# The last store of a router kernel, issued as two halves of the partitions by two engines

## The chip, the cores and the metric

The kernel runs on one core of a Trainium2 chip. The metric is the device time of one execution in microseconds; less is better. The profile's span, from the first to the last instruction of the core, is somewhat shorter than that time, because the time also holds what surrounds the program.

A core has engines with instruction streams of their own: TensorE (PE) for matrix products and transposes, VectorE (DVE), ScalarE (ACT), GpSimd (POOL) and SyncE (SP). They hand work to each other through semaphores. SyncE, ScalarE and GpSimd can issue DMA transfers between the large memory (DRAM) and the on-chip memory, which has 128 partitions. The transfers are carried out by the core's 16 DMA engines, and a transfer raises a semaphore by 16 in all when it has landed.

## The reference

A softmax over eight logits per row of a large input:

```python
# x: [16, 512, 1024] float32, router_weights: [1024, 8] float32
def reference(x, router_weights):
    logits = np.matmul(x, router_weights)
    exp_logits = np.exp(logits - np.max(logits, axis=-1, keepdims=True))
    return (exp_logits / np.sum(exp_logits, axis=-1, keepdims=True)).astype(np.float32)
```

There are 16 x 512 = 8192 rows. The input has 33.5 MB, the output 8192 x 8 floats, which is 256 KB.

## The kernel before

The 8192 rows are laid out as 128 partitions times 64 columns (`J`): partition `p` holds rows `64 p` to `64 p + 63`. So a column `j` is one row of each partition, and a partition's results for neighbouring columns are neighbours in DRAM.

```python
x_rows = x.rearrange("b s d -> (b s) d").rearrange("(p j) d -> p j d", p=P)      # P = 128
out_rows = out.rearrange("b s n -> (b s) n").rearrange("(p j) n -> p j n", p=P)  # J = 64, N = 8
...
outv = sb("outv", [P, J, N], fp32)      # all results, on chip
...
s_st = [sem(f"s_st{i}") for i in range(2)]
```

The input comes in by loads issued by GpSimd, after two issued by SyncE and the weights issued by ScalarE at the very start:

```python
nc.sync.dma_start(
    out=x_f32[:, 2 * i:2 * i + 2, :], in_=x_rows[:, 2 * i:2 * i + 2, :]
).then_inc(s_f[i], 16)                                    # line 131, i = 0 and 1
...
nc.scalar.dma_start(
    out=w8, in_=router_weights.rearrange("(ko ki) n -> ko ki n", ko=KO)
).then_inc(s_w, 16)                                       # line 137, KO = 8 rows of 4 KB
```

For each column TensorE transposes the eight 128 x 128 blocks of x, VectorE and ScalarE copy the turned blocks out of the accumulation memory, and TensorE multiplies them with the weights. The softmax is done by VectorE and ScalarE for groups of eight columns. The last four columns (`ALONE = 4`) are done one by one, so that the work after the last load is short; their sum, reciprocal and scaling are the last three instructions of VectorE. The scaling writes the last results to `outv` and raises `s_out` for the last time, to `NG + 1`.

```python
# ScalarE, at the end of its list
def power_alone(k):
    act.wait_ge(s_low, k + 1)
    act.activation(
        ev3[:, k, :], alone[k], func=Exp, bias=low[:, k:k + 1]
    ).then_inc(s_e3, 1)                                   # line 342
...
for k in range(ALONE):
    power_alone(k)

# VectorE, at the end of its list
dve.wait_ge(s_e3, ALONE)
dve.reduce_sum(sum3[:, :, 0], ev3, axis=X).then_inc(s_d, 1)               # line 441
dve.wait_ge(s_d, 3 * (NG) + 1)
dve.reciprocal(inv3, sum3).then_inc(s_d, 1)                               # line 443
dve.wait_ge(s_d, 3 * (NG) + 2)
dve.tensor_tensor(
    out=outv[:, J - ALONE:J, :], in0=ev3, in1=inv3.broadcast_to([P, ALONE, N]), op=ALU.mult
).then_inc(s_out, 1)                                                      # line 445
```

SyncE passes on, for each column, that its input has landed (line 157). After that it stores the results in two parts, and waits until both have landed. The first part is columns 0 to 51 (`DONE` = 52), the last part columns 52 to 63: 12 x 8 floats, 384 bytes, from each of the 128 partitions, 48 KB in all.

```python
sp.wait_ge(s_out, NG - 1)
sp.dma_start(out=out_rows[:, 0:DONE, :], in_=outv[:, 0:DONE, :]).then_inc(s_st[0], 16)   # line 160
sp.wait_ge(s_out, NG + 1)
sp.dma_start(out=out_rows[:, DONE:J, :], in_=outv[:, DONE:J, :]).then_inc(s_st[1], 16)   # line 162
for s in s_st:
    sp.wait_ge(s, 16)                                                                    # line 164
```

Of the kernel before, what the change touches and what calls it, by code (L numbers as in the profile page):

```python
# [11 lines left out]
def kernel(  # L12
# [7 lines left out]
    P = 128  # L20
# [5 lines left out]
    J = M // P  # L26
# [3 lines left out]
    out_rows = out.rearrange("b s n -> (b s) n").rearrange("(p j) n -> p j n", p=P)  # L30
# [15 lines left out]
    NG = (J - ALONE + SKIP) // G  # L46
    starts = [max(0, G * g - SKIP) for g in range(NG)]
    ends = [G * (g + 1) - SKIP for g in range(NG)]
    DONE = ends[-2]
# [5 lines left out]
    def sb(name, shape, dtype):  # L55
        size = mybir.dt.size(dtype)
        for n in shape[1:]:
            size *= n
        at = place[0]
        place[0] = -(-(at + size) // 64) * 64  # L60
        return nc.alloc_sbuf_tensor_at(name, shape, dtype, offset=at).ap()
# [11 lines left out]
    outv = sb("outv", [P, J, N], fp32)  # L73
# [22 lines left out]
    sem = tc.alloc_semaphore  # L96
# [23 lines left out]
    s_low = sem("s_low")  # L120
    s_e3 = sem("s_e3")
    s_out = sem("s_out")
    s_st = [sem(f"s_st{i}") for i in range(2)]

    first = [sum(LOADS[:i]) for i in range(len(LOADS))]
    cols = [sum(PIECES[:i]) for i in range(len(PIECES))]
# [2 lines left out]
    with tc.manual_schedule():  # L129
        early = [  # L130
            nc.sync.dma_start(
                out=x_f32[:, 2 * i:2 * i + 2, :], in_=x_rows[:, 2 * i:2 * i + 2, :]
            ).then_inc(s_f[i], 16)
            for i in range(2)
# [3 lines left out]
                out=w8, in_=router_weights.rearrange("(ko ki) n -> ko ki n", ko=KO)  # L138
# [8 lines left out]
    sp = nc.sync  # L147
# [11 lines left out]
    sp.wait_ge(s_out, NG - 1)  # L159
    sp.dma_start(out=out_rows[:, 0:DONE, :], in_=outv[:, 0:DONE, :]).then_inc(s_st[0], 16)  # L160
    sp.wait_ge(s_out, NG + 1)
    sp.dma_start(out=out_rows[:, DONE:J, :], in_=outv[:, DONE:J, :]).then_inc(s_st[1], 16)
    for s in s_st:
        sp.wait_ge(s, 16)

# [1 line left out]
    for i, r in enumerate(LOADS):  # L167
        if i:
            nc.gpsimd.dma_start(  # L169
                out=xa[:, first[i]:first[i] + r, :], in_=x_rows[:, first[i]:first[i] + r, :]  # L170
            ).then_inc(s_ld[i], 16)
        if i == 2:
# [3 lines left out]
                out=ident, in_=ident, compare_op=ALU.not_equal, fill=1.0, base=0,  # L176
# [151 lines left out]
    act = nc.scalar  # L328
# [11 lines left out]
# [4 lines that stand above are left out]
        ).then_inc(s_e3, 1)  # L344
# [16 lines left out]
    act.copy(xTz[0], z_bank[0]).then_inc(s_zc[0], 1)  # L361
    for k in range(ALONE):
        power_alone(k)


    dve = nc.vector
# [52 lines left out]
    for j in range(J - 3):  # L419
# [26 lines left out]
        out=outv[:, J - ALONE:J, :], in0=ev3, in1=inv3.broadcast_to([P, ALONE, N]), op=ALU.mult  # L446
# [31 lines left out]
```

## Time and profile before

| What | Value |
|---|---|
| time, median of 3 runs | 87.13 us (87.0 to 87.17) |
| span in the profile | 85.7 us |
| busy share of the span: TensorE, VectorE, ScalarE, GpSimd | 74%, 45%, 44%, 16% |
| read from and written to DRAM | 33.59 MB and 0.26 MB |
| first store: size, from issue to landing | 208 KB, 1.9 us |
| last store: size, from issue to landing | 48 KB, 1.6 us |
| DMA packets of SyncE's queue (q1) and ScalarE's queue (q10) | 576 and 16 |

The page of a profile shows the span in 40 slices with one digit for each, the busy share in tenths. "DMA" is the mean busy share of the 16 DMA engines. The chain that ended last is followed back from the last instruction. A row of a table by stretches begins with its window in microseconds and its length; then come busy time and instruction counts of TensorE's multiplier, its weight loads, VectorE, ScalarE and GpSimd, the granted clock of TensorE, the mean busy share of the DMA engines, and the rate in GB/s. "SPq" and "ACTq" are the queues of instructions of SyncE and ScalarE, in which DMA issues stand; the length of an issue is not that of the transfer. A number after L is a line of the kernel.

### The profile page before, as it was taken

Reading aid. Unit: us, or ns where it says so; the run is one execution under the profiler, and the core shown is the slowest. Engines: PE = TensorE matmul, PEld = TensorE weight load, DVE = VectorE, ACT = ScalarE, POOL = GpSimd, SP = SyncE. Lnnn points to the kernel's source line nnn. Section 1 sums busy time; section 2 is a strip of 40 time slices with the busy share of each in tenths; the row PEclk is TensorE's granted clock in tenths of the full one; section 3 lists DMA queues with packets and bytes.
Section 4 is the critical chain, followed back from the end, with each engine's and each line's share of the span. In section 5 each row is a group of like instructions: output and inputs, shape, how many; then the busy total and the mean of one; then the engine's idle time right before and its main releaser. Section 6 shows DMA issues by size and latency. Waiting matters only on the chain. (4 is left out here: it accounts for less than half of the span.)

```text
span 85.7 us, 2847 instructions
## 1 busy us (share of the span) xinstructions
PE 63.7 (74%) x1094; PEld 52.0 (61%) x1094; DVE 38.9 (45%) x114; ACT 38.1 (44%) x81; POOL 13.4 (16%) x30
## 2 busy tenths in 40 slices
PE   0052639999998986959496895959597799999860
PEld 0040637888886764838475673837475588776740
DVE  0020222447467452745256362636256267664661
ACT  0029386246556262535245252525336256555370
POOL 0489999800000000000000000000000000000000
PEclk9999999999999999999999999999999999999995
DMA  3899999999999999999999999999999999999920
GB/s 50 337 417 318 218 203 226 210 222 210 222 207 226 203 226 207 230 199 230 199 230 214 218 210 218 222 210 218 210 218 197 216 212 214 200 211 209 163 99 23
DMA packets 3906, 18.14 MB, mean 212 GB/s; under 512 B 568, under 2 KB 1080, under 8 KB 2112
## 3 DMA queue, kind: packets, MB, share of 16 engines
q0 software_dynamic: 3312, 15.73, 89.9%
q1 hardware_dynamic: 576, 2.36, 7.3%
q10 hardware_dynamic: 16, 0.03, 0.4%
q14 instruction: 2, 0.02, 0.0%
HBM read 33.59 MB, written 0.26 MB: 395 GB/s over the span
## 5 line engine op out<-in xcount | busy, mean ns | idle before, releaser
L348 ACT COPY xTs<-pts 128x384 bf16<-128x384 bf16 x63 | 30.2, 479 | 38.0 <-PE pts L276 36.7
L374 DVE COPY xTv<-ptv 128x640 bf16<-128x640 bf16 x63 | 31.0, 492 | 34.1 <-PE ptv L276 29.8
L276 PE MATMUL ptv<-identity,x_all 128*128 128x128 bf16 x311 | 28.7, 225 | 13.1 <-SPq L157 8.8
L276 PEld LDWEIGHTS ptv<-identity,x_all 128*128 (+1 forms) x311 | 18.9, 99 | 14.4 <-issue 14.3
L276 PE MATMUL pts<-identity,x_all 128*128 128x128 bf16 x186 | 21.3, 225 | 0.0
L263 PEld LDWEIGHTS lg<-w_bf,xTv 128*128 128x128 bf16 x305 | 15.6, 98 | 7.9 <-issue 1.5
L263 PE MATMUL spare<-filler 128*128 128x512 bf16 x61 | 19.5, 401 | 0.6
L263 PE MATMUL lg<-w_bf,xTv 128*128 128x8 bf16 x305 | 16.6, 167 | 0.0
L276 PEld LDWEIGHTS pts<-identity,x_all 128*128 x186 | 13.6, 101 | 0.0
L263 PE MATMUL lg<-w_bf,xTs 128*128 128x8 bf16 x183 | 13.2, 166 | 0.0
L169 POOL DMA_DIRECT2D x_all<-in_x_dram x20 | 10.7, 607 | 2.8 <-POOLq L144 2.8
L263 PEld LDWEIGHTS lg<-w_bf,xTs 128*128 128x128 bf16 x183 | 8.9, 96 | 0.0
L263 PEld LDWEIGHTS spare<-filler 128*128 128x128 bf16 x61 | 4.5, 101 | 2.5 <-issue 2.5
L270 PE MATMUL extra<-ident,w 8*128 8x8 f32 x8 | 1.0, 250 | 5.3 <-PEq L268 5.3
L270 PEld LDWEIGHTS extra<-ident,w 8*128 8x128 f32 x8 | 0.9, 198 | 5.3 <-issue 5.3
L333 ACT CAST x_all<-x_f 128x1024 bf16<-128x1024 f32 x4 | 4.0, 1044 | 0.0
L333 ACT ACT_TABLE_LOAD x1 | 1.3, 1283 | 5.9 <-ACTq L331 5.9
L382 DVE TENSOR_REDUCE mx<-lg 128x8 f32<-128x64 f32 (+1 forms) x8 | 1.8, 221 | 4.3 <-PE lg L263 4.3
L368 DVE CAST identity<-ident 128x128 bf16<-128x128 f32 x1 | 0.5, 518 | 5.2 <-POOL ident L175 5.2
L338 ACT ACTIVATE ev<-ex 128x64 f32<-128x64 f32 (+1 forms) x8 | 2.0, 253 | 1.1 <-DVE ex L386 1.0
L182 POOL DMA_DIRECT2D x_all<-in_x_dram x3 | 1.7, 697 | 0.0
L386 DVE TENSOR_TENSOR ex<-lg,mx 128x64 f32<-128x64 f32 (+1 forms) x8 | 1.7, 212 | 0.0
(40 smaller groups left out, 16.0 us busy)
## 6 DMA issues: line engine op xcount, KB each, us to landing
x_all<-in_x_dram POOLq DMA_DIRECT2D x12, 1024.0 KB, 32.5
x_f<-in_x_dram SPq DMA_DIRECT2D x2, 1024.0 KB, 6.9
x_all<-in_x_dram POOLq DMA_DIRECT2D x3, 512.0 KB, 60.3
x_all<-in_x_dram POOLq DMA_DIRECT2D x5, 256.0 KB, 64.4
out_dram<-outv SPq DMA_DIRECT2D x1, 208.0 KB, 1.9
x_all<-in_x_dram POOLq DMA_DIRECT2D x1, 128.0 KB, 66.0
x_all<-in_x_dram POOLq DMA_DIRECT2D x2, 64.0 KB, 65.7
out_dram<-outv SPq DMA_DIRECT2D x1, 48.0 KB, 1.6
```

Source lines behind the costliest of these rows:

```text
L169: nc.gpsimd.dma_start(out=xa[:, first[i]:first[i] + r, :], in_=x_rows[:, first[i]:first[i] + r, :]).then_inc(s_ld[i], 16)
L182: nc.gpsimd.dma_start(out=xa[:, J - 1, c], in_=x_rows[:, J - 1, c]).then_inc(s_z[i], 16)
L263: return pe.matmul(spare, lhsT=filler[:, 0:P], rhs=filler, start=True, stop=True)
L270: t = pe.transpose(w_ps[:, n, :], w8[:, :, n], ident[0:KO, 0:KO])
L276: turn_like = pe.transpose(turn_ap(0, 0), xa[:, 0, 0:P], identity).ins
L333: act.copy(xa[:, k, :], x_f32[:, k, :]).then_inc(s_cast, 1)
L338: act.activation(ev[g % 2][:, 0:n, :], ex[g % 2][:, 0:n, :], func=Exp).then_inc(s_ev, 1)
L348: act.copy(xTs[j % 2], pts[j % 2][:, 0:SN, :]).then_inc(s_c[j % 2], 1)
L368: dve.tensor_copy(out=identity, in_=ident).then_inc(s_idb, 1)
L374: dve.tensor_copy(out=xTv[j % 2], in_=ptv[j % 2][:, 0:VN, :]).then_inc(s_c[j % 2], 1)
L382: dve.reduce_max(mx[b][:, 0:n, 0], rows, axis=X).then_inc(s_d, 1)
L386: dve.tensor_tensor(out=ex[b][:, 0:n, :], in0=rows, in1=mx[b][:, 0:n, :].broadcast_to([P, n, N]), op=ALU.subtract,).then_inc(s_ex, 1)
```

## The change

The last store is issued as two. SyncE stores partitions 0 to 63 of the last twelve columns, ScalarE partitions 64 to 127 of the same columns, each with a semaphore of its own. ScalarE has ended its own work by then and waits for the same count of `s_out` as SyncE. SyncE waits at the end for all three stores. What is stored, and when it may be stored, stays as it was. The aim is that the two issuing engines share the work of sending the last 48 KB, which stands at the very end of the program.

```diff
-    s_st = [sem(f"s_st{i}") for i in range(2)]
+    s_st = [sem(f"s_st{i}") for i in range(3)]
...
     sp.wait_ge(s_out, NG + 1)
-    sp.dma_start(out=out_rows[:, DONE:J, :], in_=outv[:, DONE:J, :]).then_inc(s_st[1], 16)
+    sp.dma_start(
+        out=out_rows[0:P // 2, DONE:J, :], in_=outv[0:P // 2, DONE:J, :]
+    ).then_inc(s_st[1], 16)
     for s in s_st:
         sp.wait_ge(s, 16)
...
     for k in range(ALONE):
         power_alone(k)
+    act.wait_ge(s_out, NG + 1)
+    act.dma_start(
+        out=out_rows[P // 2:P, DONE:J, :], in_=outv[P // 2:P, DONE:J, :]
+    ).then_inc(s_st[2], 16)
```

## The prediction

> **What bounds the kernel now.** I read the page first, then the chain that ended last, then what the queue of SyncE waited for, then the timeline of the last microseconds, and at the end a table by stretches that I cut myself. The page says what sets the pace of the body: the DMA share is 9 tenths in nearly every slice and falls only in the last two.
>
> ```profile
> DMA  3899999999999999999999999999999999999920
> GB/s 50 337 417 318 218 203 226 210 222 210 222 207 226 203 226 207 230 199 230 199 230 214 218 210 218 222 210 218 210 218 197 216 212 214 200 211 209 163 99 23
> ```
>
> So the body waits for the input loads, and the change touches none of them. What it touches lies in the last slices, after the input has come. There the chain of waits is a single file from engine to engine; its last steps are these (start us, length us, what):
>
> ```profile
> 82.89 0.18 DVE low L410
> 83.06 0.02 issue
> 83.09 0.28 ACT ev L342
> 83.36 0.02 issue
> 83.39 0.20 DVE sum L441
> 83.58 0.02 issue
> 83.61 0.19 DVE inv L443
> 83.80 0.02 issue
> 83.82 0.19 DVE outv L445
> ```
>
> The reader should see two things. Each hand-over costs 0.02 us, and the list stops at 84.01 us, while the span is 85.7 us. What follows is the last store, which the chain does not count as engine work. The timeline has it:
>
> ```profile
> 84.04 0.34 SPq L162 DMA_DIRECT2D out_dram<-outv  x1
> ```
>
> And the waits of SyncE's queue (waited for: us, times, longest):
>
> ```profile
> SPq L164 <- DMA out_dram<-outv: 1.2, 1, 1.2
> ```
>
> Line 162 is the last store: its issue takes 0.34 us, and then SyncE waits 1.2 us in line 164 for it to land. That is 84.04 to about 85.63, some 1.6 us at which every compute engine is idle. I cut this stretch by trial at the first and last moment at which the DMA engines move anything:
>
> ```profile
> core 0: us, PE busy (x) PEld busy (x) DVE busy (x) ACT busy (x) POOL busy (x), PEclk, DMA share, GB/s
> 84.04:84.38 0.34, 0.00 (x0) 0.00 (x0) 0.00 (x0) 0.00 (x0) 0.00 (x0) 0.50 0.00 0
> 84.38:84.88 0.50, 0.00 (x0) 0.00 (x0) 0.00 (x0) 0.00 (x0) 0.00 (x0) 0.50 0.00 0
> 84.88:85.19 0.31, 0.00 (x0) 0.00 (x0) 0.00 (x0) 0.00 (x0) 0.00 (x0) 0.50 0.59 159
> 85.19:85.66 0.47, 0.00 (x0) 0.00 (x0) 0.00 (x0) 0.00 (x0) 0.00 (x0) 0.50 0.00 0
> ```
>
> This is the whole case in four rows: 0.34 us of issue, 0.50 us in which nothing moves yet, 0.31 us with packets, 0.47 us between the last packet and the end. Only 0.31 of the 1.62 us moves bytes. In it an engine is busy 0.59 x 0.31 = 0.18 us on average; the rest is that engines start and stop at different moments.
>
> **How far the fixed parts depend on size.** The earlier store, line 160, moves 208 KB against 48 KB with the same 128 pieces of one partition each. Its issue took the same 0.34 us (81.03). The same cut for it gives no store packet from 81.38 to 81.87, then packets to 82.57. So issue (0.34) and the gap (0.49 against 0.50) are fixed in bytes, and only the moving part grew, from 0.31 to 0.70 us for 160 KB more, 2.4 ns per KB.
>
> **What the Trainium skill says.** Three places bear on this.
>
> "DMA: Bandwidth & Descriptors", section "Rules for kernel authors", has a row on two transfers to disjoint partition halves and says of it "Don't bother", because both halves spread over all 16 DMA engines and share them. Its section "Issuing engines are not separate DMA queues" says the same of DMAs from several engines: only the issuing time can be saved. No trace here has a split store yet; that the moving part is but 0.31 us agrees in so far as there is little to save.
>
> The same page, "Why a DMA increments its semaphore by 16 and not by 1", lets a transfer use the largest number of engines up to 16 that divides the outer size; 64 partitions still give 16. The trace agrees with its counting: in the stretch from 84 us the DMA view has 144 packets, which is 128 pieces and 16 semaphore writes, and the weights load of 8 rows shows 16 packets on ScalarE's queue, 8 and 8.
>
> "Perfetto Trace Analysis", section "DMA Instruction — HWDGE (DVE, Sync)", says that the reported length of an issue includes the wait for a descriptor generator that is locked for exclusive use. Whether SyncE and ScalarE can hold it at once is the open question of this case. The only place here where both issue together is the start:
>
> ```profile
> 0.74 0.58 ACTq L137 DMA_DIRECT2D w<-in_router_weights_dram  x1
> 0.74 0.86 SPq L131 DMA_DIRECT2D x_f<-in_x_dram  x2
> ```
>
> ScalarE's one issue, of only 8 rows, took 0.58 us, and SyncE's two took 0.38 and 0.42 us (the view of line 131), against 0.34 us when SyncE issues alone. All are longer than alone, ScalarE's by 0.24 us. It may be the lock, a dearer issue on ScalarE, or a cold start.
>
> **The change part by part.**
>
> 1. Removed: half of SyncE's pieces, 64 of 128. By size, 24 KB less at 2.4 ns is 0.06 us on that queue. But the halves go to the same 16 engines, each with 4 + 4 pieces in place of 8, so the sum of bytes and pieces on each engine is as before. Moving part: 0 us saved if the two run interleaved.
> 2. Issue on SyncE: I leave it at 0.34 us. The issue did not follow the bytes, and the issue of 8 rows was not shorter than one of 128, so I see no reason for 64 to be shorter. 0 us.
> 3. Making the pieces in two places at once: the mean engine is busy 0.18 us within a moving part of 0.31 us, so 0.13 us is spread between engines. If that comes from pieces being made one after another, halves made side by side would halve it: up to -0.06 us.
> 4. Added on ScalarE: a wait for the last result and one issue. ScalarE ends its last exponential at 83.36, so it stands ready; the hand-over is the usual 0.02 us and it starts at 84.04 beside SyncE. It costs the path nothing if it takes 0.34 us; if it takes the 0.58 us of the start, its gap and packets end 0.24 us later.
> 5. In that late case the half behind moves alone, 4 pieces per engine: half of the 0.18 us busy time, 0.09 us, is already done. Net +0.24 - 0.09 = +0.15 us.
> 6. Added: 16 semaphore writes of 4 bytes, one per engine, and a third semaphore for SyncE to wait for. Most wait instructions of SyncE's list took 17 ns (the view of line 157). I put +0.02 us for both.
>
> Sums: side by side, -0.06 + 0.02 = -0.04 us; with ScalarE late, +0.15 + 0.02 = +0.17 us. The 0.50 us gap and the 0.47 us after the last packet stay in both cases, because each half has to go through its own.
>
> **The rivals.**
>
> (a) The split gains: two generators work side by side, the spread falls, and even the gap gets shorter because it holds the making of the first 128 pieces. Against it: the gap was the same 0.49 to 0.50 us for both stores, and I have no trace of a 64-partition store. Worth at most about -0.2 us if both spread and part of the issue halve: 86.95.
>
> (b) Hidden either way, the transfers interleave on the same engines: 87.1.
>
> (c) ScalarE's issue becomes the last thing: +0.15 to +0.25 us, 87.3 to 87.4. For it speaks the 0.58 us at the start; against it, that this was the first instruction of the program, and with another shape.
>
> (d) The halves run one after another as whole stores. A second full issue, +0.34 us, behind a locked generator, gives 87.45. The start speaks against: SyncE's first issue began at the same 0.74 us and took only 0.38.
>
> No case reaches 2%, which is 1.74 us: the whole tail after the last result is 1.62 us, and a gain would have to remove all of it. A loss of that size would need a second tail behind the first, and nothing makes one store wait for the other.
>
> **Range and chances.** I give about a half to no loss (a and b, around -0.04 us) and a half to a late ScalarE (c and d, around +0.2 us). The mean of the two is +0.08 us, so 87.13 + 0.08 is 87.2 us. The runs before lie within 87.0 to 87.17, so I allow about 0.1 us for the draw on either side of the cases: 86.9 to 87.5. Chances: faster by over 2% 0.01, within 2% 0.98, slower by over 2% 0.01.
>
> **What would show it.** In the changed profile the two issues should stand beside each other at the time of the last result plus 0.02 us. SyncE's at 0.34 us means step 2 holds; ScalarE's near 0.34 or near 0.58 decides between (b) and (c); a start at the same moment but a length near 0.7 would be (d). The packets on SyncE's queue should be 576 - 64 = 512, on ScalarE's 16 + 64 + 16 = 96. The stretch with packets should be about 0.25 to 0.3 us if side by side, and near 0.45 us if staggered; the gap and the last 0.47 us should be as before. The prediction is wrong if the gap or the last stretch moves, if an issue of 64 partitions costs clearly less than 0.34 us, or if the time moves through the part before 84 us, which none of my steps touches.

## The result, and the profile after

The time went from 87.06 to 88.06 us (medians of six runs each, 86.95 to 87.17 and 87.46 to 88.47): a ratio of 1.0104, with a 95% interval of 1.0062 to 1.0146. The change costs about one per cent, 1.0 us, on a tail of 1.62 us. The forecast was 87.2 us with a range up to 87.5.

The timeline after has the two issues side by side, at the moment at which they were expected, 0.03 us after the last result:

```profile
84.05 0.19 DVE L451 TENSOR_TENSOR outv<-ev,inv 128x32 f32<-128x32 f32 x1
84.27 0.55 SPq L162 DMA_DIRECT2D out_dram<-outv  x1
84.27 0.56 ACTq L367 DMA_DIRECT2D out_dram<-outv  x1
```

The reader should look at the lengths. Each engine sends half of what SyncE sent before, and each takes 0.55 us for it where SyncE took 0.34 for the whole. The waits of SyncE's queue show the wait for the stores, now two of them:

```profile
SPq L166 <- DMA out_dram<-outv: 1.5, 2, 1.3
```

The issues with their sizes, and the time from issue to landing, in the DMA view:

```profile
out_dram<-outv SPq DMA_DIRECT2D x1, 24.0 KB, 1.8
out_dram<-outv ACTq DMA_DIRECT2D x1, 24.0 KB, 2.1
```

Half the bytes take 1.8 and 2.1 us to land, the whole took 1.6. The table by stretches, cut as in the prediction where packets begin and end:

```profile
84.27:84.82 0.55, 0.00 (x0) 0.00 (x0) 0.00 (x0) 0.00 (x0) 0.00 (x0) 0.50 0.00 0
84.82:85.46 0.64, 0.00 (x0) 0.00 (x0) 0.00 (x0) 0.00 (x0) 0.00 (x0) 0.50 0.00 0
85.46:85.73 0.27, 0.00 (x0) 0.00 (x0) 0.00 (x0) 0.00 (x0) 0.00 (x0) 0.50 0.35 91
85.73:86.01 0.28, 0.00 (x0) 0.00 (x0) 0.00 (x0) 0.00 (x0) 0.00 (x0) 0.50 0.34 88
86.01:86.40 0.39, 0.00 (x0) 0.00 (x0) 0.00 (x0) 0.00 (x0) 0.00 (x0) 0.50 0.00 0
```

The four rows of before (0.34, 0.50, 0.31, 0.47) have become five. Issue is 0.21 us longer, the gap to the first packet 0.14 longer, and the packets come in two batches, one after the other: the rows of 0.27 and 0.28 us each have a DMA share of about 0.35, that is 0.09 us of work per engine. By their queues, the first batch is SyncE's and the second ScalarE's. So the moving part is 0.55 us for the bytes that took 0.31. Only the last row is shorter, by 0.08. Sum of the differences: 0.21 + 0.14 + 0.24 - 0.08 = 0.51 us, from 1.62 to 2.13.

The other half of the loss is elsewhere. The spans of the changed kernel's six runs have a median of 86.35 us; those of 31 runs of the kernel before, taken later, 85.7. That is +0.65, of which the tail explains 0.51. The rest lies before the tail: the last result came at 84.24 us in this profile and at 84.01 in that of before. In the kernels below that keep everything up to the last result, the issue began anywhere between 84.03 and 84.23 us, and at 84.08 in the one that puts ScalarE off, which is the changed kernel up to that point. So this is taken for the draw of the loads; 84.27 is the latest of all, and that the change has no part in it is not shown. And the time less the span, what lies outside the program, was 1.65 us (median of six) against 1.33. Two of the six runs had 1.34 and 1.36 us, four had 1.63 to 1.79. That is +0.3 us in a place where the prediction had nothing.

### The profile page after: what moved, and what is told of

Same layout as the page of the kernel before. It is cut to its first block, busy times and chain, and to the rows that moved or that the text cites. A ratio compares the mean times of both kernels' runs of the same rounds, so it can differ in the third digit from the quotient of the medians.

```text
span 86.4 us, 2849 instructions
## 1 busy us (share of the span) xinstructions
PE 63.0 (73%) x1094; PEld 51.4 (60%) x1094; DVE 38.9 (45%) x114; ACT 38.1 (44%) x81; POOL 13.4 (16%) x30
## 5 line engine op out<-in xcount | busy, mean ns | idle before, releaser
L265 PE MATMUL spare<-filler 128*128 128x512 bf16 x61 | 19.0, 393 | 0.7
```

What stands on the lines that cost most here:

```text
L265: return pe.matmul(spare, lhsT=filler[:, 0:P], rhs=filler, start=True, stop=True)
```

## The experiments

Three theories at the start: two issues that begin together hinder each other; a store of 64 partitions is dear by itself; ScalarE's issues are dear.

**Half a store alone.** SyncE keeps its half, the other is not stored.

```diff
-    sp.dma_start(out=out_rows[:, DONE:J, :], in_=outv[:, DONE:J, :]).then_inc(s_st[1], 16)
+    sp.dma_start(
+        out=out_rows[0:P // 2, DONE:J, :], in_=outv[0:P // 2, DONE:J, :]
+    ).then_inc(s_st[1], 16)
```

> SyncE stores partitions 0 to 63 of the last columns, alone; the other half of the last results is left out and not stored. Theory 1 (two issues that begin together hinder each other): the issue is back at 0.34 us, the gap from its end to the first packet at 0.50, and the tail is a little shorter than before, about 1.5 us; time 87.0. Theory 2 (a store of 64 partitions is itself dearer to issue than one of 128): the issue stays at 0.55 us and the gap near 0.65, time about 87.3. Theory 3 (ScalarE's issue is slow by itself and SyncE only suffers from it) expects what theory 1 does here.

It took 87.37 us, ratio 1.0053 (1.0032 to 1.0073): leaving out half of the last results makes the kernel slower. In the table by stretches of this kernel, the rows from the issue to the end of the packets:

```profile
84.08:84.63 0.55, 0.00 (x0) 0.00 (x0) 0.00 (x0) 0.00 (x0) 0.00 (x0) 1.00 0.00 0
84.63:85.28 0.65, 0.00 (x0) 0.00 (x0) 0.00 (x0) 0.00 (x0) 0.00 (x0) 1.00 0.00 0
85.28:85.55 0.27, 0.00 (x0) 0.00 (x0) 0.00 (x0) 0.00 (x0) 0.00 (x0) 1.00 0.35 91
```

No second engine issues anything here, and issue and gap are exactly as long as in the changed kernel. The half is dear by itself.

**Both halves by SyncE, one after the other.**

```diff
+    for h in range(2):
+        rows = slice(h * P // 2, (h + 1) * P // 2)
+        sp.dma_start(
+            out=out_rows[rows, DONE:J, :], in_=outv[rows, DONE:J, :]
+        ).then_inc(s_st[1 + h], 16)
```

> Both halves, both issued by SyncE, one after the other. Theory 1: 0.34 us each, so the second issue ends 0.34 us later than the whole store's did, less about 0.1 us for the 4 pieces per engine that have moved by then: +0.25 us, time 87.3. Theory 2: two issues of 0.55 us, last packet some 0.9 us later than before, time about 87.9. Theory 3: as theory 1.

88.08 us, ratio 1.0127 (1.0097 to 1.0158). The two issues took 553 and 580 ns: the second theory again, without ScalarE. In the timeline they stand as one row:

```profile
84.19 1.18 SPq L164 DMA_DIRECT2D out_dram<-outv  x2
```

**The whole store by ScalarE.**

```diff
+    act.wait_ge(s_out, NG + 1)
+    act.dma_start(out=out_rows[:, DONE:J, :], in_=outv[:, DONE:J, :]).then_inc(s_st[1], 16)
```

> The whole last store of 128 partitions, issued by ScalarE alone; SyncE only waits. Theory 1: an issue of about 0.34 us and a gap of 0.50 as on SyncE, time within 0.1 us of before, 87.1. Theory 3: an issue of 0.55 us or more and a longer gap, time 87.4 to 88. Theory 2: as theory 1. Should the time rise by more than the span does, ScalarE's late end costs something after the last instruction.

```profile
84.23 0.39 ACTq L363 DMA_DIRECT2D out_dram<-outv  x1
```

The issue took 0.39 us, the gap 0.50, the moving part 0.31: within 0.05 us of SyncE's, so ScalarE's issue is not what is dear. Yet the time was 87.36 us, ratio 1.0037 (1.0026 to 1.0048), while the spans had a median of 85.8 against 85.7. The time less the span was 1.56 us, between 1.52 and 1.65 in all 13 runs.

**Two engines, cut by columns.** Each stores all 128 partitions, six columns.

```diff
+    MID = DONE + 6
+    sp.dma_start(out=out_rows[:, DONE:MID, :], in_=outv[:, DONE:MID, :]).then_inc(s_st[1], 16)
...
+    act.wait_ge(s_out, NG + 1)
+    act.dma_start(out=out_rows[:, MID:J, :], in_=outv[:, MID:J, :]).then_inc(s_st[2], 16)
```

> Two stores by the two engines at the same moment, as in the change, but split by columns: each has all 128 partitions and 6 columns, 24 KB as in the change. Theory 1: both issues at 0.55 us or more, and since each has twice the pieces of a half, the second's first packet comes even later; time 88.0 to 88.4. Theory 2: issues of 0.34 us, time about 87.2. Theory 3: SyncE's issue 0.34, ScalarE's 0.55, time 87.4.

87.38 us, ratio 1.0037 (1.0019 to 1.0054). The timeline:

```profile
84.17 0.34 SPq L163 DMA_DIRECT2D out_dram<-outv  x1
84.17 0.39 ACTq L366 DMA_DIRECT2D out_dram<-outv  x1
```

Same bytes per engine, same moment, twice the pieces, and both issues are as short as when each engine is alone. That does away with the first theory for the issue.

**ScalarE's half alone.** SyncE's half is left out of the changed kernel.

> ScalarE stores partitions 64 to 127 of the last columns, alone; partitions 0 to 63 of these columns are left out. In the changed kernel ScalarE's first packet came 1.47 us after its issue began, SyncE's 1.20, which is also what SyncE's half took alone. If the extra 0.27 us came from two halves being prepared one after the other, ScalarE's half alone has its first packet 1.20 to 1.25 us after its issue begins and the time is as with SyncE's half alone, 87.4 to 87.6. If it is ScalarE's own, it stays at 1.47 us and the time is 87.7 or more.

87.63 us, ratio 1.0062 (1.0045 to 1.0079).

```profile
84.09 0.53 ACTq L363 DMA_DIRECT2D out_dram<-outv  x1
```

The first packet came 1.18 us after the beginning of this issue. So the 1.47 us in the changed kernel (84.27 to 85.73) is not ScalarE's own: 0.29 us of it is that the other half goes first.

**The changed kernel with ScalarE put off by a copy of 0.48 us.**

```diff
     act.wait_ge(s_out, NG + 1)
+    act.copy(xTs[0], pts[0][:, 0:SN, :]).then_inc(s_a, 1)
+    act.wait_ge(s_a, 1)
     act.dma_start(
```

> The changed kernel with ScalarE's half put off by one copy of 0.48 us after the last result. In the changed kernel its first packet came 1.47 us after its issue began, alone 1.18. If its descriptors have to wait for those of the other half, then begun 0.5 us later they wait no more: first packet 1.18 to 1.25 us after its issue begins, and the span grows by only some 0.2 us over the changed kernel. If two halves in one program hinder each other in some other way, it stays near 1.47 us.

One run, 88.28 us. The timeline, and the stretch with ScalarE's packets:

```profile
84.08 0.55 SPq L163 DMA_DIRECT2D out_dram<-outv  x1
84.59 0.53 ACTq L370 DMA_DIRECT2D out_dram<-outv  x1
85.78:86.05 0.27, 0.00 (x0) 0.00 (x0) 0.00 (x0) 0.00 (x0) 0.00 (x0) 1.00 0.35 91
```

ScalarE's packets began 1.19 us after its issue: begun 0.51 us after the other half, it does not queue. Its span, 86.4 us, looks like that of the changed kernel, but only because its last result came 0.19 us earlier. From SyncE's issue to the end it took 2.36 us (84.08 to 86.44) where the changed kernel took 2.13. Of the 0.51 us by which ScalarE was put off, 0.28 is the queueing that it no longer meets, and 0.23 us is lost.

**What makes 64 partitions dear.** Six kernels change the shape of SyncE's one last store, in the place of the first diff, and leave out what it does not cover.

> SyncE stores partitions 0 to 63 in two pieces each (columns 52 to 56 and 58 to 62), so 64 partitions but 128 pieces; columns 57 and 63, and partitions 64 to 127 of the last twelve columns, are left out. If the dear issue follows from the count of partitions, it stays at 0.55 us or grows; if it is the count of pieces being below 128, it falls back to 0.34 us.

> SyncE stores partitions 0 to 95 of the last columns; the other 32 are left out. If every store on fewer than 128 partitions is dear, the issue is 0.55 us and the first packet 1.2 us after its beginning. If the cost follows the count, it lies between 0.34 and 0.55 us, near 0.45.

> SyncE stores partitions 0 to 79 of the last columns; the other 48 are left out. Stores of 96 and 128 partitions were issued in 0.36 and 0.34 us, one of 64 in 0.55. If the dear form begins at 64 partitions and below, this one takes 0.36 us with its first packet after 0.86; if the cost follows 64 alone, the same; if it begins somewhere between 64 and 96, it may take 0.55.

> SyncE stores partitions 0 to 31 of the last columns; the other 96 are left out. If 64 partitions and below are the dear form, the issue takes 0.55 us or somewhat more or less; if 64 alone is dear, 0.34 to 0.36 us.

> SyncE stores partitions 0 to 47 of the last columns; the other 80 are left out. If 64 is special among the counts, the issue takes 0.36 us with the first packet after 0.86. If something else than the count decides, it may take 0.55.

> SyncE stores partitions 0 to 63 of columns 52 to 59 only, pieces of 256 bytes in place of 384; columns 60 to 63 and partitions 64 to 127 of the last twelve are left out. If 64 partitions are dear whatever the size, 0.55 us and first packet after 1.20; if it is the pairing of 64 with pieces of 384 bytes, 0.36 us and 0.86.

| last store by SyncE | issue, us | first packet after the issue begins, us |
|---|---|---|
| 128 partitions (the kernel before) | 0.34 | 0.85 |
| 96 | 0.36 | 0.85 |
| 80 | 0.36 | 0.86 |
| 64 | 0.55 | 1.20 |
| 64, pieces of 256 bytes | 0.55 | 1.20 |
| 64, two pieces each | 0.73 | 1.37 |
| 48 | 0.36 | 0.85 |
| 32 | 0.36 | 0.85 |

The guess that the cost begins at some count below 128 is wrong: counts on either side of 64 are cheap, and pieces of 256 bytes are as dear as pieces of 384. Nor does it matter which half it is: the second issue of both halves by SyncE was for partitions 64 to 127, and as dear. Of the counts tried, 64 alone is dear, and more pieces from each of the 64 made it dearer. These are single profiles, but apart from the row of two pieces the two groups lie 0.2 and 0.35 us apart and agree within 0.02 us inside. Compare these rows of the store of 32 partitions with those of half a store above:

```profile
84.04:84.40 0.36, 0.00 (x0) 0.00 (x0) 0.00 (x0) 0.00 (x0) 0.00 (x0) 1.00 0.00 0
84.40:84.89 0.49, 0.00 (x0) 0.00 (x0) 0.00 (x0) 0.00 (x0) 0.00 (x0) 1.00 0.00 0
84.89:85.11 0.22, 0.00 (x0) 0.00 (x0) 0.00 (x0) 0.00 (x0) 0.00 (x0) 0.57 0.23 56
```

**The change with the cut moved.** If 64 is the cause, the same change cut at 96 must lose much less.

```diff
-        out=out_rows[0:P // 2, DONE:J, :], in_=outv[0:P // 2, DONE:J, :]
+        out=out_rows[0:96, DONE:J, :], in_=outv[0:96, DONE:J, :]
...
-        out=out_rows[P // 2:P, DONE:J, :], in_=outv[P // 2:P, DONE:J, :]
+        out=out_rows[96:P, DONE:J, :], in_=outv[96:P, DONE:J, :]
```

> The change with the cut moved: SyncE stores partitions 0 to 95, ScalarE 96 to 127, at the same moment. Stores of 96 and of 32 partitions had cheap issues (0.36 us, first packet after 0.86). If 64 partitions are the cause, both issues take 0.36 to 0.40 us, the tail is within 0.2 us of the kernel before, and the time is 87.2 to 87.4, as with the split by columns. If two engines at once are the cause, the issues take 0.55 us and the time is 88.

87.36 us, ratio 1.0042 (1.0027 to 1.0057). The timeline:

```profile
84.03 0.36 SPq L162 DMA_DIRECT2D out_dram<-outv  x1
84.04 0.40 ACTq L367 DMA_DIRECT2D out_dram<-outv  x1
```

The loss falls from 1.04% to 0.42%. The tail was 1.79 us, 0.17 over before; the packets took 0.36 us (before 0.31), and the stretch after them 0.56 (before 0.47). Of the 0.51 us of the changed kernel's tail, 0.34 thus goes with the count of 64 and 0.17 with two stores on two engines; the cut by columns, with a tail of 1.77 us, says much the same. In the times the shares are about 0.6% and 0.4%, less certain, because the change's own interval runs from 0.6 to 1.5% and the time outside the span is mixed in.

**The time outside the span.** ScalarE's list goes on in the changed kernel for 1.25 us after its last exponential, 0.7 us of it waiting for the last result. To see whether that wait alone costs something, it waits here and issues nothing.

```diff
+    act.wait_ge(s_out, NG + 1).then_inc(s_a, 1)
```

> The kernel before, with ScalarE waiting for the last result and issuing nothing, so that it ends its list at 84.1 us in place of 83.4. The time less the span was 1.33 us before and 1.56 us where ScalarE issued the whole store. If ScalarE's late end costs that, the time less the span is about 1.5 us here and the time 87.2 to 87.3; if it is the transfer on ScalarE's queue, it stays at 1.33 and the time at 87.06.

87.07 us, ratio 0.9997 (0.9989 to 1.0006), time less span 1.31 us. A ScalarE that waits to the last result costs nothing. With other last stores the number changes:

| kernel | last stores | time less span, us: median (lowest to highest), runs |
|---|---|---|
| before, four comparisons | SyncE, 128 partitions | 1.27 to 1.37 in 83 of 89 runs, 1.70 to 1.85 in six |
| ScalarE waits only | SyncE, 128 | 1.31 (1.27 to 1.35), 12 |
| whole store by ScalarE | ScalarE, 128 | 1.56 (1.52 to 1.65), 13 |
| ScalarE's half alone | ScalarE, 64 | 1.63 (1.62 to 1.65), 4 |
| SyncE's half alone | SyncE, 64 | 1.37 (1.29 to 1.90), 9 |
| both halves by SyncE | SyncE, 64 twice | 1.48 (1.40 to 1.57), 4 |
| cut by columns | both, 128 | 1.47 (1.29 to 1.84), 14 |
| cut at 96 | both, 96 and 32 | 1.36 (1.34 to 1.87), 5 |
| changed kernel | both, 64 | 1.65 (1.34 to 1.79), 6 |

Where ScalarE has a last store to itself, every run pays some 0.2 to 0.3 us. With a store on each engine, or SyncE's half alone, a run pays either nothing or 0.3 to 0.6: four of the changed kernel's six runs do, two of five cut at 96, seven of 14 cut by columns, four of nine with SyncE's half, and six of 89 of the kernel before.

No instruction of the core stands there, but the DMA view goes on beyond the span. In the changed kernel, between 86.4 and 90 us, it has one packet, which begins at 87.92 us, and in the kernel before, from 85.7 us on, none:

```profile
q14 instruction: 1, 0.01, 0.6%
DMA packets 0, 0.00 MB, mean 0 GB/s; under 512 B 0, under 2 KB 0, under 8 KB 0
```

Such a packet of 8 KB, on the queue that the view calls instruction, stands 1.3 to 1.6 us after the end of the span in seven of the 18 profiles: the changed kernel, the one that puts ScalarE off, the four others with SyncE's last stores on 64 partitions, and the first of the two versions below. In these seven runs the time exceeds the span by 1.45 to 1.84 us. Nine of the other eleven have 1.32 or 1.33 us; the remaining two, those with ScalarE's store alone, have 1.59 and 1.60 without such a packet. So the packet goes with the surplus wherever SyncE has a last store. What calls it up, and whether it is the cause or a companion, was not tried; ScalarE's surplus comes without it.

**Two versions meant to be faster.** The tables of stretches say that on 128 partitions issue and gap are fixed, and that the moving part follows the bytes. So the last store should be small, on 128 partitions. First with a third store, for the group that is done near 83.2 us:

```diff
+    sp.wait_ge(s_out, NG)
+    sp.dma_start(
+        out=out_rows[:, DONE:J - ALONE, :], in_=outv[:, DONE:J - ALONE, :]
+    ).then_inc(s_st[2], 16)
     sp.wait_ge(s_out, NG + 1)
-    sp.dma_start(out=out_rows[:, DONE:J, :], in_=outv[:, DONE:J, :]).then_inc(s_st[1], 16)
+    sp.dma_start(out=out_rows[:, J - ALONE:J, :], in_=outv[:, J - ALONE:J, :]).then_inc(s_st[1], 16)
```

> A version meant to be faster: the last store is cut by columns and in time, not by partitions. Columns 52 to 59 are stored by SyncE as soon as they are done, near 83.2 us, on all 128 partitions; only the last four columns, 16 KB in pieces of 128 bytes, are stored at the end. By the 2.4 ns per KB of the two stores before, 32 KB less save 0.08 us, less 0.02 us for the third semaphore: 87.0. If the store issued 0.85 us earlier is still being moved when the last one begins, or hinders its issue, there is a loss of 0.1 to 0.2 us.

The tail did shrink, to 1.56 us (84.12 to 85.68), but the ratio was 1.0005 (0.9988 to 1.0023; medians 87.21 and 87.06): no difference that can be measured. The time less the span rose to 1.50 us, with one transfer more on SyncE's queue; and the ratio still flatters it, since four of the 19 runs before in this comparison were among the six with 1.70 us and more. Then the same without a further transfer, by moving the border between the two stores:

```diff
-    DONE = ends[-2]
+    DONE = ends[-1]
...
-    sp.wait_ge(s_out, NG - 1)
+    sp.wait_ge(s_out, NG)
```

> A version meant to be faster, with two stores as before but the border moved: the first store takes columns 0 to 59 and is issued when these are done, near 83.2 us; the last takes the last four columns, 16 KB, with 128 partitions. No further transfer and no further semaphore. The first store's packets should run from 84.04 to about 84.8 and be gone when those of the last begin at 84.9: span 0.06 to 0.08 us shorter, time less span as before, time 87.0. If the first store's packets are still moving then, the gain is lost or turns to +0.1 us.

86.93 against 87.02 us, ratio 0.9992 (0.9985 to 0.9999), time less span 1.33 us. The rows of this kernel's tail:

```profile
84.10:84.45 0.35, 0.00 (x0) 0.00 (x0) 0.00 (x0) 0.00 (x0) 0.00 (x0) 1.00 0.76 291
84.45:84.96 0.51, 0.00 (x0) 0.00 (x0) 0.00 (x0) 0.00 (x0) 0.00 (x0) 1.00 0.77 282
84.96:85.19 0.23, 0.00 (x0) 0.00 (x0) 0.00 (x0) 0.00 (x0) 0.00 (x0) 1.00 0.48 72
85.19:85.63 0.44, 0.00 (x0) 0.00 (x0) 0.00 (x0) 0.00 (x0) 0.00 (x0) 1.00 0.00 0
```

The first store now fills the issue and the gap of the second (DMA share 0.76 and 0.77 where there was 0.00), and the moving part is 0.23 us in place of 0.31. This is the fastest of the versions that store everything, by 0.08%, with an interval that just misses 1.

## Why the prediction was wrong

The direction was right and so was "within 2%", but the direction by luck: the forecast's rise of 0.08 us came from a long issue on ScalarE at the start of the program, a cost that a whole store from ScalarE did not have. The range was missed by 0.56 us. By its steps:

- **What bounds the end, and the four rows: right.** The tail is where the change's loss inside the span arose; the rest is the draw of the loads and what lies outside the span. SyncE's queue had 512 packets and ScalarE's 96, as counted, so the work per engine is what the prediction said.
- **Step 2, "Issue on SyncE: I leave it at 0.34 us": this failed.** It took 0.55. The argument was that the issue follows neither the bytes nor the count of rows. It asked only whether a half could be cheaper. Two stores of 128 partitions, equal in form, can't show what another count costs, and the one issue with another count, that of 8 rows with its 0.58 us, was put down to lock, engine or cold start. The shape was named once, in rival (c), and not followed. Whether 8 rows are dear as 64 are was not tried.
- **"The 0.50 us gap ... stay": failed with it.** The gap was 0.64 us, and that it moves was one of the prediction's own signs of being wrong. Step 2 and the gap together are +0.35 us of the tail's +0.51.
- **Steps 1 and 3, halves made side by side, up to -0.06 us: wrong in sign.** The halves of 64 come one behind the other, against the prediction's "nothing makes one store wait for the other"; the moving part went from 0.31 to 0.55. Nor does half the work take half the time: one half's packets alone took 0.27 us, where those of the whole took 0.31. With 128 partitions on each engine, in the cut by columns, the overlap is real: the packets took 0.36 us in all.
- **Step 4: the start right, the reason wrong.** ScalarE began with SyncE, and 0.56 us was close to the 0.58 allowed for. But a whole store took it 0.39 us: the length came from the count, not from the engine or the start of the program.
- **Step 5, a late ScalarE at +0.15 us net:** both were late. Against SyncE's packets ScalarE's were later by 0.27 us. The deduction of 0.09 us for work already done failed for the reason just given: a half that moves alone takes nearly as long as a whole. Only the last stretch was shorter (-0.08).
- **Rival (d) was the nearest.** The halves do run one after another, though not by one issue being held: both issues overlap in full at the length that they have alone (0.55 and 0.56 us, alone 0.55 and 0.53), and the order shows only in the packets. It gave 87.45 us because it had the fixed parts at their old size.
- **What no step had:** the 0.3 us between span and time. The prediction carried the sums of the tail straight over to the time, and so took what lies outside the span as fixed.

## What to carry to other kernels

A last store like this one is paid almost wholly in fixed parts (1.3 of 1.62 us), so cutting it among engines has little to save; what helped here, and by no more than 0.08%, was to let it carry few bytes on all 128 partitions and to send the rest early enough to hide in its issue and gap. Before a transfer is cut by partitions, look at the length of its issue in a profile for the very count that the cut makes; a neighbouring count is no evidence. And when a tail is tuned by tenths of a microsecond, compare times as well as spans, since another set of transfers may cost something after the last instruction.

## What the runs showed of the hardware

A last store of 64 partitions took 0.53 to 0.58 us to issue, from either engine, and when alone 1.18 to 1.20 us from the beginning of the issue to its first packet. When alone, stores of 32, 48, 80, 96 and 128 took 0.33 to 0.39 us and 0.83 to 0.89 us. Issued by ScalarE beside one of SyncE's, stores of 128 and 32 took 0.39 and 0.40 us, and 0.93 and 0.99 us to their first packets. Cutting each of the 64 rows into two pieces made the issue 0.73 us. Two stores of 64 issued together by the two engines send their packets one batch after the other, the second 0.27 us later; begun 0.51 us apart they do not hinder each other. Why 64 is treated apart stays open; it was seen for stores of this one layout only, and other counts were not tried. A last store issued by ScalarE was followed by 1.52 to 1.65 us outside the span where the same store from SyncE was, in most runs, followed by 1.27 to 1.37; the cause of that stays open too. In the profiles where SyncE had a last store, a time outside the span of 1.45 us and more went with a late packet of 8 KB on the instruction queue (seven of seven), and one of 1.32 or 1.33 us with none (nine of nine).
